# A two-block network on one core: the feed-forward norm's factor applied behind the second projection, rotary on wide tiles, no splits on GpSimd, a later merge, and the modulation rows spread differently

## The chip, the core and the metric

The kernel is one program on one core of one Trainium2 chip. The metric is the device time of one execution in microseconds (us), lower is better. The reported time is the median of the runs shown. One execution was also taken by the profiler; its own time and its span (first to last instruction) stand beside the median in the table below.

## What is computed

All tensors are float32, the sequence has 256 tokens and the width is 1024. Two networks follow each other.

```
# first block, twice (i = 0, 1)
z = rmsnorm(h, norm1[i]) @ w_in[i]                     # 1024 x 2560
q, k = partial rotary of the first 16 of 64 dims of each of 12 heads
h += concat(pool_mixer(u), dilated_attention(q, k, v)) @ w_out[i]
h += square(relu(rmsnorm(h, norm2[i]) @ w_up[i])) @ w_down[i]      # 1024 -> 4096 -> 1024
h += sigmoid(rmsnorm(h, norm3[i]) @ w_gate[i]) * (p[i] @ w_ple[i])
x = rmsnorm(h, final_norm)
# second block
mod   = silu(c)     @ w_mod + b_mod      # six parts of 1024: shifts, scales, gates
mod_c = silu(c_ctx) @ w_mod + b_mod      # only its parts 0 and 1 are used
h, hc = modulated norms of x (latent) and ctx (context), each @ w_in
context: gated delta rule in chunks of 64, both directions -> states
latent:  the same from these states -> o
merged = gate0 * (norm(o)*silu(z)) @ w_dn_out + gate1 * short_conv @ w_sc_out + gate2 * fourier @ w_fn_out
x += g1 * merged @ w_o
x += g2 * swiglu(modulated norm of x)
out = rmsnorm(x, final)
```

Since relu(r*y)^2 = r^2 * relu(y)^2 for r > 0, a norm's factor r of a token may be applied before the square, or as r^2 = 1/(mean square + eps) to the token's column of the second projection's result.

## The kernel before

**Products.** Float32 accuracy comes from splits: a matrix is cut into a high part in fp32r and the rest (`wh`, `wl` for weights, `xh`, `xl` for activations), and a product is three matmuls (`mm3`: high-high, high-rest, rest-high). A weight unit is 128 x 1024 (512 KB). `weights` (L250) loads it on SyncE's queue into `wst` (3 buffers), makes `wh` on ScalarE (L262) and `wl` on VectorE (L263), each as two halves of 512 columns. While `self.onpool` is above zero `wl` is made on GpSimd instead; the mixer sets it to `np2` = 3, so the first three weights of the mixer, six halves, go there. One unit feeds 24 matmuls of 256 columns.

**Order.** The program is written in one order, and the tile framework's list scheduler builds each engine's instruction stream from it: the traced order is the priority, an instruction that the scheduler's own model finds ready may be put ahead of earlier ones, and a tile needs a free buffer. Each engine then runs its stream strictly in order. `issue_after` puts an edge from an instruction to those traced in its block. A second stream is woven into the first by hand: `beside(gen, rate)` registers a generator, and each `tick` (one for each weight unit in `cols_into`, L664 and L672, and in a few other places) adds `rate` to a credit and takes one step of the generator for each whole credit. `drain` takes all that is left at once.

**Stages.** For i = 0, 1: attention (`proj`, `rotate`, `scores`, `softmax`, `av`, `pool`; no ticks), `ple`, the output projection `row_tiles`, `residual` (L699), `ffn(i)` (L706) and `gate(i)`. Then the mixer: value, query and key inputs of context and latent, `branches`, `dn_output`, the output products; then `swiglu` and `finish`.

**Feed-forward.** `ffn` splits h times its gain (`norm_split`, L297 and L298) without the norm's factor, so the first product can start at once. Meanwhile the factor's row is made in steps: the sum of squares (`sumsq`, ScalarE and VectorE), after the first unit the column sums on TensorE and a reciprocal root of ten small VectorE instructions (L345 to L361), after the third unit a transpose to a row `nrow`. From then on each pair of units f = 0..15 goes through `square`: relu and factor in one VectorE instruction for each half (L716), two squares on ScalarE (L719, L720), the rest on VectorE (L721). The second projection `down` runs one pair behind. At the end `residual` adds the four accumulators (256 columns x 2) to h in five VectorE instructions (L704), and `gate` begins with its own `norm_split` of h.

**Modulation.** `modulation` loads one 512 KB tile of `w_mod` (L878, pool `mp`, two buffers) and forms its row sums with one VectorE instruction of 1024 columns for each vector (L882): two vectors for parts 0 and 1, one for parts 2 to 5; eight tiles and nine steps for a part. Parts (1, 0, 2) are registered beside the first feed-forward at rate 0.85; parts (3, 4, 5) beside the latent's key and value inputs in the mixer at rate 0.8, and what is left there is woven with the recurrence. Its instructions carry an edge behind the last `shifted` one traced before, if there is one.

**Context and recurrence.** `context` runs beside the second feed-forward at rate 1.2, `recurrence` beside the branches at rate 0.8. In both, `dn_base` inverts 16 x 16 blocks on GpSimd, with trips through DRAM before and after (`there`, `back`, `xc`), then yields `self.trip` = 10 times, and `dn_merge` takes the result up (L1317, `Tm` and `U`).

Of the kernel before, what the change touches and what calls it, by code (L numbers as in the profile page):

```python
# [9 lines left out]
F32 = mybir.dt.float32  # L10
F32R = mybir.dt.float32r
I32 = mybir.dt.int32
AF = mybir.ActivationFunctionType
# [3 lines left out]
P = 128  # L17
# [177 lines left out]
def run(g):  # L195
    for _ in g:
        pass
# [33 lines left out]
class Net:  # L231
# [218 lines left out]
    def rotary(self):  # L450
# [28 lines left out]
        nc.scalar.activation(self.cos, t, AF.Sin)  # L479

# [29 lines left out]
    def rotate(self, z):  # L510
        nc = self.nc
        zz = z.rearrange("p t (h d) -> p t h d", d=HD)
        x1, x2 = zz[:, :, :, 0:8], zz[:, :, :, 8:16]
        co = self.cos[:, :, None, :].to_broadcast([P, 2, 8, 8])
        si = self.sin[:, :, None, :].to_broadcast([P, 2, 8, 8])
        w = [self.b1.tile([P, 2, 8, 8], F32, name=f"rot{j}", bufs=1) for j in range(4)]
        for o, x, c in zip(w, (x1, x2, x2, x1), (co, si, co, si)):
            for t in range(2):
                nc.vector.tensor_mul(o[:, t], x[:, t], c[:, t])
        for t in range(2):  # L520
            nc.vector.tensor_sub(x1[:, t], w[0][:, t], w[1][:, t])
            nc.vector.tensor_add(x2[:, t], w[2][:, t], w[3][:, t])
# [176 lines left out]
    def residual(self, acc):  # L699
        h = self.h  # L700
        for j in range(4):
            for n in ((0, 1), (1, 2)) if j == 3 else ((0, 2),):
                js = slice(2 * j + n[0], 2 * j + n[1])
                self.nc.vector.tensor_add(h[:, js], h[:, js], acc[j][:, n[0]:n[1]])  # L704

    def ffn(self, i):  # L706
        nc = self.nc
# [4 lines left out]

        def square(bv):
            t = self.sm.tile([P, 2, T], F32, name="fft", tag="w2k", bufs=self.nw2k)
            for n in range(2):
                nc.vector.scalar_tensor_tensor(t[:, n], bv[:, n], 0.0, r[0], op0=OP.max, op1=OP.mult)  # L716
            ah = self.sm.tile([P, 2, T], F32R, name="ah", tag="w2k", bufs=self.nw2k)
            al = self.sm.tile([P, 2, T], F32R, name="al", tag="w2k", bufs=self.nw2k)
            nc.scalar.activation(ah, t, AF.Square)  # L719
# [3 lines left out]

        r = []
        steps = self.row_steps_sb(self.h, r)
        next(steps)
        wait = []
        for f in range(16):
            bv = self.bank2()
            if f == 0 and self.ko & 4:  # L730
                self.cols_into(bv, [self.a["w_up"][i, n] for n in range(2)], x, True)
            for n in range(2):
                if f or not self.ko & 4:
                    self.cols_into(bv[:, n:n + 1], [self.a["w_up"][i, 2 * f + n]], x)
                if f == self.at[0] and n == self.at[1]:
                    next(steps)
                if f == self.at[2] and n == self.at[3]:
                    run(steps)
                    for b in wait:
                        square(b)  # L740
                    wait = None
            if wait is not None:
                wait.append(bv)
            else:
                square(bv)
                while len(pend) > 1:
                    down(False)
        self.residual(down(True))
# [57 lines left out]
    def layer(self, i):  # L806
# [38 lines left out]
        if i == 0:  # L845
            self.mod_setup()
            self.beside(self.modulation(*self.mod_parts[0]), 0.85)
# [72 lines left out]
    def context(self, d, e):  # L920
# [17 lines left out]
        yield from self.modulate(Halves(hc), self.gains[:, 1], self.mod[:, 0, 1], x)  # L938
# [836 lines left out]
    def run(self):  # L1775
# [5 lines left out]
        self.np1 = 3  # L1781
        self.np2 = 3
# [31 lines left out]
        self.trip = 10  # L1814
        self.mod_parts = (((1, 0, 2), (3,), (4, 5)), ((1, 0, 2), (), (3, 4, 5)), ((1, 0, 2, 3), (), (4, 5)), ((1, 0), (), (2, 3, 4, 5)))[1]
# [47 lines left out]
```

## Time and profile before

| | |
|---|---|
| median of 3 runs | 1226.24 us (1225.2 to 1228.88) |
| the profiled execution | 1224.34 us, span 1222.2 us |
| mean granted TensorE clock | 0.986 of full speed |
| TensorE busy, of the span | 1174.3 us, 96% |
| VectorE busy | 899.3 us, 74% |
| ScalarE busy | 635.6 us, 52% |
| GpSimd busy | 119.9 us, 10% |

How to read it: the busy time of an engine is the union of its instructions' intervals. A matmul's interval is longer than the distance to the next one, since they overlap, so a TensorE that is called busy can still run below its best rate; how many matmuls start in a stretch, and at which granted clock, says more.

### The profile page before, as it was taken

How to read it: one execution, taken by the hardware profiler on the slowest of the kernel's cores; microseconds unless marked ns; L12 is line 12 of the kernel's file. 1: busy time of each engine (PE TensorE's matmuls, PEld its weight loads, DVE VectorE, ACT ScalarE, POOL GpSimd, SP SyncE). 2: the span in 40 equal slices, each digit the busy share in tenths (PEclk: the TensorE clock that was granted, in tenths of full speed). 3: DMA queues.
4: the chain of work that ended last, by engine and by line, in shares of the span. 5: the costliest groups of instructions: out<-in, count | busy, mean ns of one | idle time of the engine just before them, and what ended most of it. 6: DMA issues, size and time to landing. Idle time of an engine off the chain costs nothing.

```text
span 1222.2 us, 24807 instructions
## 1 busy us (share of the span) xinstructions
PE 1174.3 (96%) x9882; PEld 1111.4 (91%) x9882; DVE 899.3 (74%) x1804; ACT 635.6 (52%) x1250; POOL 119.9 (10%) x207
## 2 busy tenths in 40 slices
PE   8999899999999989999999999997999999999997
PEld 6779899999977889999999979897989998999996
DVE  6998997556998488675657899897655768555555
ACT  5654645545755565644445555544333546544444
POOL 1000000000010000064000130275000000000000
PEclk9999999999999999999999989999999998999998
DMA  6767688555553645556444525677422452655552
GB/s 223 238 199 249 208 297 278 189 194 190 164 174 121 200 139 164 182 165 207 156 147 164 171 91 164 226 270 243 142 89 100 173 195 99 213 185 189 186 180 84
DMA packets 65779, 221.43 MB, mean 181 GB/s; under 512 B 10048, under 2 KB 11456, under 8 KB 65664
## 3 DMA queue, kind: packets, MB, share of 16 engines
q1 hardware_dynamic: 64800, 218.29, 53.4%
q0 software_dynamic: 864, 1.57, 0.6%
q8 instruction: 77, 1.26, 0.4%
q14 instruction: 38, 0.31, 0.1%
HBM read 218.00 MB, written 1.84 MB: 180 GB/s over the span
## 4 chain that ended last, share of the span: by engine, by line
PE 72%; DVE 13%; DMA 6%; POOL 4%; issue 3%; ACT 2%; SPq 0%; DVEq 0%; POOLq 0%; ACTq 0%
PE acc L274 38%; PE bank L274 33%; DVE wl L263 4%; DMA wmst<-w_mod 2%; DVE xl L298 1%; POOL bo L1288 1%; POOL bz L1289 1%; ACT wh L262 1%; DVE wmst L882 1%; PE bank L565 1%; DVE h L704 1%; DVE cy L1044 1%; DMA back<-bzt 1%; DVE qkT L533 1%; DMA pt<-pT 0%
## 5 line engine op out<-in xcount | busy, mean ns | idle before, releaser
L262 ACT ACTIVATE wh<-wst 128x512 fp32r<-128x512 f32 x708 | 411.9, 624 | 427.4 <-PE bank L274 157.3
L263 DVE TENSOR_TENSOR wl<-wst,wh 128x512 fp32r<-128x512 f32 x702 | 470.1, 703 | 208.5 <-ACT wh L262 208.0
L274 PE MATMUL bank<-xl,wh 128*128 128x256 f32 x992 | 280.5, 283 | 2.1 <-DVE xl L298 2.1
L274 PE MATMUL bank<-xh,wl 128*128 128x256 f32 x992 | 279.4, 282 | 2.9 <-DVE wl L263 2.9
L274 PE MATMUL bank<-xh,wh 128*128 128x256 f32 x992 | 281.3, 284 | 0.8 <-ACT wh L262 0.8
L274 PE MATMUL acc<-al,wh 128*128 128x256 f32 x688 | 191.6, 279 | 0.0
L274 PE MATMUL acc<-ah,wl 128*128 128x256 f32 x688 | 191.3, 279 | 0.0
L274 PE MATMUL acc<-ah,wh 128*128 128x256 f32 x688 | 191.2, 279 | 0.0
L274 PEld LDWEIGHTS bank<-xh,wl 128*128 128x128 f32 x992 | 187.0, 189 | 4.3 <-DVE wl L263 4.3
L274 PEld LDWEIGHTS bank<-xl,wh 128*128 128x128 f32 x992 | 187.0, 189 | 2.8 <-DVE xl L298 2.7
L274 PEld LDWEIGHTS bank<-xh,wh 128*128 128x128 f32 x992 | 187.1, 189 | 1.6 <-ACT wh L262 1.2
L274 PE MATMUL acc<-xh,wh 128*128 128x256 f32 x640 | 183.4, 287 | 2.2 <-ACT xh L911 2.2
L274 PE MATMUL acc<-xl,wh 128*128 128x256 f32 x640 | 182.0, 285 | 1.5 <-DVE xl L912 1.5
L274 PE MATMUL acc<-xh,wl 128*128 128x256 f32 x640 | 181.1, 284 | 0.5 <-DVE wl L263 0.4
L274 PEld LDWEIGHTS acc<-al,wh 128*128 128x128 f32 x688 | 129.0, 188 | 0.0
L274 PEld LDWEIGHTS acc<-ah,wl 128*128 128x128 f32 x688 | 128.9, 188 | 0.1
L274 PEld LDWEIGHTS acc<-ah,wh 128*128 128x128 f32 x688 | 128.9, 188 | 0.0
L274 PEld LDWEIGHTS acc<-xh,wh 128*128 128x128 f32 x640 | 121.6, 190 | 4.7 <-ACT xh L911 2.8
L274 PEld LDWEIGHTS acc<-xl,wh 128*128 128x128 f32 x640 | 121.5, 190 | 2.9 <-DVE xl L912 1.7
L274 PEld LDWEIGHTS acc<-xh,wl 128*128 128x128 f32 x640 | 121.9, 191 | 1.5 <-DVE wl L263 0.9
L274 PE MATMUL acc<-wl,xh 128*128 128x512 f32 x176 | 70.6, 401 | 2.5 <-DVE wl L263 2.4
L274 PE MATMUL acc<-wh,xh 128*128 128x512 f32 x176 | 70.8, 406 | 1.1 <-ACT wh L262 1.1
(365 smaller groups left out, 1564.8 us busy)
## 6 DMA issues: line engine op xcount, KB each, us to landing
wst<-w_up SPq DMA_DIRECT2D x64, 512.0 KB, 4.2
wst<-w_down SPq DMA_DIRECT2D x64, 512.0 KB, 4.2
wmst<-w_mod SPq DMA_DIRECT2D x48, 512.0 KB, 4.8
wst<-w_fin SPq DMA_DIRECT2D x44, 512.0 KB, 3.2
wst<-w_in SPq DMA_DIRECT2D x39, 512.0 KB, 3.6
wst<-w_mgate SPq DMA_DIRECT2D x24, 512.0 KB, 3.3
wst<-w_fout SPq DMA_DIRECT2D x22, 512.0 KB, 3.2
wst<-w_qkv SPq DMA_DIRECT2D x20, 512.0 KB, 3.4
```

What stands on the lines that cost most here:

```text
L262: nc.scalar.activation(wh[:, c:c + n], st[:, c:c + n], AF.Copy)
L263: i = (nc.gpsimd if self.onpool > 0 else nc.vector).tensor_tensor(wl[:, c:c + n], st[:, c:c + n], wh[:, c:c + n].bitcast(F32), op=OP.subtract)
L274: self.nc.tensor.matmul(out, lhsT, rhs, start=start, stop=stop, skip_group_check=skip)
L298: nc.vector.scalar_tensor_tensor(xl[:, k], src, gain, xh[:, k].bitcast(F32), op0=OP.mult, op1=OP.subtract)
L533: nc.vector.tensor_copy(qk[:, :, t * P:(t + 1) * P], bk.rearrange("p (c q) -> p c q", c=4))
L565: nc.tensor.transpose(bk[:, c * P:(c + 1) * P], s[:, g, c * P:(c + 1) * P], self.ident)
L704: self.nc.vector.tensor_add(h[:, js], h[:, js], acc[j][:, n[0]:n[1]])
L882: nc.vector.scalar_tensor_tensor(pr, st, 1.0, cv[v], op0=OP.mult, op1=OP.mult, accum_out=mod[:, part, v, k:k + 1])
L1044: nc.vector.scalar_tensor_tensor(y4[:, j], pad[:, j, :, tap:tap + CHUNK], w[:, j, tap:tap + 1], y4[:, j], op0=OP.mult, op1=OP.add)
L1288: pool.tensor_tensor(o, lt[:, c:, j:c].to_broadcast([P, n, c]), Z[:, j:c, 0:c].to_broadcast([P, n, c]), op=OP.mult)
L1289: pool.tensor_tensor(Z[:, c:, 0:c], Z[:, c:, 0:c], o, op=OP.subtract)
```

## The change

It does these things:

- `ffn` applies relu alone, on ScalarE, one instruction of 512 columns from PSUM; the squares and the rest are as before. The norm's steps start at f = 1 (sum of squares), 3 (mean square plus eps and its reciprocal) and 5 (transpose and copy to a row), and `residual` multiplies each accumulator by that row on VectorE before it adds.
- `rotary` builds two wide tables of 16 x 2 x 8 with eight VectorE instructions; `rotate` becomes three instructions of 256 columns in place of twelve of 64.
- `np2` is 0: no `wl` on GpSimd. (`np1` is read nowhere.)
- Modulation parts (1, 0, 2, 3) beside the first feed-forward at rate 0.55, parts (4, 5) behind the context, none in the mixer.
- `context` takes its sum of squares in its first step and then waits four steps before the rest of its norm.
- `trip` is 13.

```
--- before.py
+++ after.py
@@ -477,6 +477,13 @@
         nc.vector.scalar_tensor_tensor(t, r, -1.0, r, op0=OP.mult, op1=OP.max)
         nc.vector.tensor_scalar(t, t, -1.0, math.pi / 2, op0=OP.mult, op1=OP.add)
         nc.scalar.activation(self.cos, t, AF.Sin)
+        full = [self.b1.tile([P, 16, 2, 8], F32, name=n, bufs=1) for n in ("fcos", "fsin")]
+        for i in range(2):
+            for x in range(2):
+                for o, src, f in zip(full, (self.cos, self.sin), (1.0, 2.0 * x - 1.0)):
+                    nc.vector.tensor_scalar(o[:, 8 * i:8 * i + 8, x], src[:, i][:, None, :].to_broadcast([P, 8, 8]), f, None,
+                                            op0=OP.mult)
+        self.cos, self.sin = full
 
     def tokens_into(self, pt, x, q, w):
 
@@ -508,18 +515,13 @@
         return (z, r) if first else z
 
     def rotate(self, z):
-        nc = self.nc
-        zz = z.rearrange("p t (h d) -> p t h d", d=HD)
-        x1, x2 = zz[:, :, :, 0:8], zz[:, :, :, 8:16]
-        co = self.cos[:, :, None, :].to_broadcast([P, 2, 8, 8])
-        si = self.sin[:, :, None, :].to_broadcast([P, 2, 8, 8])
-        w = [self.b1.tile([P, 2, 8, 8], F32, name=f"rot{j}", bufs=1) for j in range(4)]
-        for o, x, c in zip(w, (x1, x2, x2, x1), (co, si, co, si)):
-            for t in range(2):
-                nc.vector.tensor_mul(o[:, t], x[:, t], c[:, t])
-        for t in range(2):
-            nc.vector.tensor_sub(x1[:, t], w[0][:, t], w[1][:, t])
-            nc.vector.tensor_add(x2[:, t], w[2][:, t], w[3][:, t])
+
+        nc = self.nc
+        zz = z.rearrange("p t (h d) -> p (t h) d", d=HD)[:, :, 0:16].rearrange("p n (x j) -> p n x j", x=2)
+        co, si = (self.b1.tile([P, 16, 2, 8], F32, name=f"rot{j}", bufs=1) for j in range(2))
+        nc.vector.tensor_mul(co, zz, self.cos)
+        nc.vector.tensor_mul(si, zz[:, :, ::-1], self.sin)
+        nc.vector.tensor_add(zz, co, si)
 
     def scores(self, i, b, z, S):
 
@@ -696,56 +698,61 @@
 
         return down
 
-    def residual(self, acc):
+    def residual(self, acc, row=None):
+
         h = self.h
         for j in range(4):
             for n in ((0, 1), (1, 2)) if j == 3 else ((0, 2),):
                 js = slice(2 * j + n[0], 2 * j + n[1])
-                self.nc.vector.tensor_add(h[:, js], h[:, js], acc[j][:, n[0]:n[1]])
+                a = acc[j][:, n[0]:n[1]]
+                if row is not None:
+                    t = self.t2k("fft")[:, n[0]:n[1]]
+                    self.nc.vector.tensor_mul(t, a, row[:, None, :].to_broadcast([P, n[1] - n[0], T]))
+                    a = t
+                self.nc.vector.tensor_add(h[:, js], h[:, js], a)
+
+    def mean_square_steps(self, h, res):
+
+        nc = self.nc
+        ss = self.sumsq(h)
+        yield
+        v = self.sm.tile([P, 2], F32, name="rsv2")
+        nc.vector.tensor_scalar(v, self.col_sums((ss,)), 1.0 / D, EPS, op0=OP.mult, op1=OP.add)
+        nc.vector.reciprocal(v, v)
+        yield
+        r = self.sm.tile([P, T], F32, name="nrow")
+        nc.scalar.activation(r, self.across(v)[:, 0:T], AF.Copy)
+        res.append(r)
 
     def ffn(self, i):
+
         nc = self.nc
         x = self.norm_split(self.h, lambda k: self.g2[:, i, k:k + 1])
         pend = []
 
         down = self.downward(self.a["w_down"][i], 32, pend)
-
-        def square(bv):
+        r = []
+        steps = self.mean_square_steps(self.h, r)
+        for f in range(16):
+            bv = self.bank2()
+            if f == 0 and self.ko & 4:
+                self.cols_into(bv, [self.a["w_up"][i, n] for n in range(2)], x, True)
+            else:
+                for n in range(2):
+                    self.cols_into(bv[:, n:n + 1], [self.a["w_up"][i, 2 * f + n]], x)
+            if f in (1, 3, 5):
+                next(steps, None)
             t = self.sm.tile([P, 2, T], F32, name="fft", tag="w2k", bufs=self.nw2k)
-            for n in range(2):
-                nc.vector.scalar_tensor_tensor(t[:, n], bv[:, n], 0.0, r[0], op0=OP.max, op1=OP.mult)
             ah = self.sm.tile([P, 2, T], F32R, name="ah", tag="w2k", bufs=self.nw2k)
             al = self.sm.tile([P, 2, T], F32R, name="al", tag="w2k", bufs=self.nw2k)
+            nc.scalar.activation(t, bv, AF.Relu)
             nc.scalar.activation(ah, t, AF.Square)
             nc.scalar.activation(t, t, AF.Square)
             nc.vector.tensor_sub(al, t, ah.bitcast(F32))
             pend.append((ah, al))
-
-        r = []
-        steps = self.row_steps_sb(self.h, r)
-        next(steps)
-        wait = []
-        for f in range(16):
-            bv = self.bank2()
-            if f == 0 and self.ko & 4:
-                self.cols_into(bv, [self.a["w_up"][i, n] for n in range(2)], x, True)
-            for n in range(2):
-                if f or not self.ko & 4:
-                    self.cols_into(bv[:, n:n + 1], [self.a["w_up"][i, 2 * f + n]], x)
-                if f == self.at[0] and n == self.at[1]:
-                    next(steps)
-                if f == self.at[2] and n == self.at[3]:
-                    run(steps)
-                    for b in wait:
-                        square(b)
-                    wait = None
-            if wait is not None:
-                wait.append(bv)
-            else:
-                square(bv)
-                while len(pend) > 1:
-                    down(False)
-        self.residual(down(True))
+            if f:
+                down(False)
+        self.residual(down(True), r[0])
 
     def ple(self, i):
         nc = self.nc
@@ -844,7 +851,7 @@
             return
         if i == 0:
             self.mod_setup()
-            self.beside(self.modulation(*self.mod_parts[0]), 0.85)
+            self.beside(self.modulation(*self.mod_parts[0]), 0.55)
         self.ffn(i)
         if self.stop == ("ffn", i):
             return
@@ -935,7 +942,11 @@
         nc.vector.tensor_scalar(self.k["dn_conv"], self.k["dn_conv"], 0.5, None, op0=OP.mult)
         yield
         x = self.xc = []
-        yield from self.modulate(Halves(hc), self.gains[:, 1], self.mod[:, 0, 1], x)
+        norm = self.modulate(Halves(hc), self.gains[:, 1], self.mod[:, 0, 1], x)
+        next(norm)
+        for _ in range(4):
+            yield
+        yield from norm
         yield
         yield from self.dn_inputs(x, True, d, e, ("k",), self.bank2)
         while d["late"]:
@@ -1778,8 +1789,8 @@
         self.side, self.rate, self.credit, self.busy = None, 0.0, 0.0, False
         self.dn_rate = 0.8
         self.hp = 0
-        self.np1 = 3
-        self.np2 = 3
+        self.np1 = 0
+        self.np2 = 0
         self.gadd = 0
         self.onpool = 0
         self.sy = 0
@@ -1811,8 +1822,8 @@
         self.ctx_rate = 1.2
         self.scan_rate = 1.8
         self.mod_rate = 0.8
-        self.trip = 10
-        self.mod_parts = (((1, 0, 2), (3,), (4, 5)), ((1, 0, 2), (), (3, 4, 5)), ((1, 0, 2, 3), (), (4, 5)), ((1, 0), (), (2, 3, 4, 5)))[1]
+        self.trip = 13
+        self.mod_parts = ((1, 0, 2, 3), (4, 5), ())
         with ExitStack() as ctx:
             self.ctx = ctx
             self.mp = ctx.enter_context(tc.tile_pool(name="mp", bufs=2, side="left"))
```

## Rows read from the trace of the kernel before

**Rows 1.** The page, part 1: busy time, share of the span, instructions.

```profile
PE 1174.3 (96%) x9882; PEld 1111.4 (91%) x9882; DVE 899.3 (74%) x1804; ACT 635.6 (52%) x1250; POOL 119.9 (10%) x207
```

**Rows 2.** Busy time by stretch: us, each engine (instructions), TensorE clock, DMA share, GB/s.

```profile
118.00:146.00 28.00, 23.62 (x185) 22.20 (x185) 26.95 (x60) 17.31 (x33) 0.00 (x0) 1.00 0.61 217
150.00:300.00 150.00, 149.57 (x1283) 149.36 (x1283) 103.66 (x183) 78.41 (x136) 0.00 (x0) 1.00 0.69 230
303.00:313.00 10.00, 9.54 (x81) 9.31 (x80) 9.72 (x21) 8.54 (x18) 0.00 (x0) 1.00 0.20 71
438.00:456.00 18.00, 13.98 (x100) 13.04 (x100) 17.04 (x50) 12.17 (x26) 0.00 (x0) 0.91 0.35 119
...
689.00:720.00 31.00, 25.91 (x190) 22.88 (x190) 26.94 (x63) 16.27 (x39) 16.81 (x30) 0.89 0.29 93
760.00:780.00 20.00, 17.09 (x121) 15.74 (x120) 17.38 (x43) 12.83 (x39) 1.37 (x4) 0.91 0.67 216
...
842.00:858.00 16.00, 10.26 (x118) 9.73 (x117) 9.21 (x21) 5.25 (x10) 3.28 (x4) 0.79 0.53 165
```

**Rows 3.** Waits of TensorE's matmuls: who for whom, us, times, longest.

```profile
PE bank L274 <- DVE U L1317: 5.4, 1, 5.4
...
PE bank L274 <- DVE rsy L358: 3.4, 1, 3.4
PE bank L370 <- DVE rsy L361: 3.1, 2, 1.9
PE bank L1143 <- DVE tokk L1134: 2.8, 1, 2.8
```

**Rows 4.** Timeline of VectorE at the first feed-forward's end: start, us, instruction.

```profile
307.33 0.74 DVE L704 TENSOR_TENSOR h<-h,acc 128x256 f32<-128x256 f32 x2
307.99 1.72 DVE L298 SCALAR_TENSOR_TENSOR xl<-h,k_norm,xh 128x256 fp32r<-128x256 f32 x4
309.62 0.69 DVE L317 TENSOR_TENSOR ssp<-sq 128x512 f32<-128x512 f32 x1
310.23 0.69 DVE L263 TENSOR_TENSOR wl<-wst,wh 128x512 fp32r<-128x512 f32 x1
```

**Rows 5.** Groups of instructions by line: count, busy us, mean ns, idle before.

```profile
L716 DVE SCALAR_TENSOR_TENSOR fft<-bank,nrow 128x256 f32<-128x256 f32 x64 | 24.4, 419 | 21.7 <-PE bank L274 21.4 <-ACT nrow L404 0.2
...
L519 DVE TENSOR_TENSOR rot<-zqk,rcos 128x64 f32<-128x64 f32 x24 | 5.3, 221 | 0.9 <-ACT zqk L507 0.8
...
L766 ACT ACTIVATE ple<-bank 128x512 f32<-128x512 f32 x8 | 4.8, 595 | 7.2 <-PE bank L274 7.2
```

**Rows 6.** Timeline of VectorE at the mixer's start.

```profile
694.56 0.16 DVE L359 SCALAR_TENSOR_TENSOR rst<-rsy 128x4 f32<-128x4 f32 x1
694.76 1.23 DVE L360 TENSOR_TENSOR rst<-rst,lv 128x4 f32<-128x4 f32 x1
...
714.17 2.88 DVE L1084 SCALAR_TENSOR_TENSOR vj<-cth,cy 128x256 f32<-128x256 f32 x2
```

**Rows 7.** Timeline of GpSimd at the mixer's start.

```profile
711.65 5.12 POOL L263 TENSOR_TENSOR wl<-wst,wh 128x512 fp32r<-128x512 f32 x2 [3.34 <-ACT wh L262]
```

**Rows 8.** Modulation tiles alone, by stretch: VectorE, ScalarE, clock, DMA share, GB/s.

```profile
60.00:118.00 58.00, 22.98 (x37) 0.00 (x0) 1.00 0.65 216
...
700.00:860.00 160.00, 30.51 (x48) 0.00 (x0) 0.95 0.59 197
```

**Rows 9.** The chain that ended last, around 759 us: start, us, what.

```profile
759.36 6.04 DMA wst<-w_z
```

**Rows 10.** The same chain between 838 and 858 us.

```profile
839.13 6.61 DMA back<-bzt
...
852.86 3.68 PE bank L274 x64
```

**Rows 11.** Timeline of ScalarE when the latent's recurrence has ended.

```profile
942.60 0.28 ACT L1123 ACTIVATE hsq<-acc 128x128 f32<-128x128 f32 x1 [2.99 <-PE acc L274]
```

**Rows 12.** Timeline of VectorE where that result is next multiplied.

```profile
973.44 1.41 DVE L1541 SCALAR_TENSOR_TENSOR do<-bank,k_onorm,zs 128x512 f32<-128x512 f32 x2 [1.46 <-PE bank L1539]
```

## The prediction, made before the change was built

> **What bounds the kernel now.** I read the page's busy times first: TensorE is busy 1174 of 1222.2 us, VectorE 74%, ScalarE 52% [rows 1]. So a VectorE instruction that goes is worth nothing in itself; only the places where TensorE stands still, or runs at a lower granted clock, can give time back. Next I read busy time by stretch to find these places [rows 2]. The reader should take one pitch from the steady feed-forward: 1283 matmuls start in 150 us, one each 0.117 us, so a weight unit of 24 takes 2.8 us. Held against that, 118 to 146 us has 185 matmuls, worth 21.6 us, in 28: 6.4 us lost. By the same sum 438 to 456 loses 6.3, 689 to 720 loses 8.8, and 760 to 780 loses 5.9. From 842 to 858 many matmuls are smaller, so there I read the idle time (16 − 10.26 = 5.7 us) and the clock, 0.79. All five stretches are touched by the change; in 150 to 300, where TensorE is busy 149.57 of 150 us, nothing is to be had. Third, TensorE's waits say what came last in these gaps: the merge's `U` 5.4 us, the column sums behind `rsy` at L358 3.4, the square root's end at L361 3.1 in two waits, and the token copy at L1134 2.8 [rows 3].
>
> **The change part by part.** The sum is made on the profiled execution's own 1224.34 us (span 1222.2 and 2.1 around it); the median of the runs is 1.9 above it, which is added at the end.
>
> 1. *Start of the second feed-forward.* The norm's ten small VectorE steps and the context's own wait behind each other in VectorE's queue (17.04 busy of 18 us), and TensorE waits 3.4 us there for `rsy` [rows 2, 3]. The change makes the row from two VectorE instructions, nothing in the first product needs it, and the context takes its norm four steps later. The wait can go, and with it the clock's loss, (1 − 0.91) × 18 = 1.6. Bounds −5.6 and −3.4 (the wait alone, without the 0.6 of idle time that is left and the clock); I take −5.
>
> 2. *Start of the first feed-forward.* TensorE idles 4.4 of 28 us at full clock [rows 2]. Of it the shorter of the L361 waits, 3.1 − 1.9 = 1.2 [rows 3], goes for certain; the rest stands behind VectorE (26.95 of 28 busy) and may go with eight instructions fewer. I take −2.5, between −1.2 and −4.4.
>
> 3. *End of each feed-forward.* `residual` gains a multiplication for each of its five adds. None like it is in the trace; the nearest rows are 0.37 for 128x256 (0.74 for two) and 0.69 for 128x512 [rows 4]. Both halves of the last accumulator give 0.74, all five 3 × 0.69 + 0.74 = 2.8. They stand ahead of the gate's split on a VectorE that is 9.72 of 10 us busy [rows 2]. What is late next is `xl` of the gate, then its first matmuls. I take +2.3 at each end, +4.6 together; at best the first four run while TensorE is at the last accumulator (0, since the adds are there now too), at worst 2.8 at each end, with a clock loss as in term 1: 2 × (2.8 + 1.6) = +8.8.
>
> 4. *Relu on ScalarE.* The 64 VectorE instructions of 0.419 us go; 32 on ScalarE come, which I price by the other ScalarE eviction of 128x512 from PSUM, 0.595 [rows 5]. ScalarE is busy 78 of 150 us [rows 2]; 32 × 0.595 = 19 us over two feed-forwards of some 165 us take it from 52% to 58%. TensorE covers it: 0. The Trainium skill has a rule against this edit: ScalarE: Activation LUTs, Rules for kernel authors, says to put relu on VectorE and not on ScalarE, since VectorE is up to about three times faster in bf16. No row here is in bf16; in float32 from PSUM the rows show 0.595 against 2 × 0.419 = 0.84, in ScalarE's favour. By the rows this term is 0; by the rule it would cost time, and that is a rival below.
>
> 5. *Rotary.* Twelve instructions of 128x64 at 0.22 become three of 128x256; 0.43 is the row for that width with two inputs [rows 4, 5]: 2.65 − 1.29 = 1.4 less at each of six calls. TensorE hardly waits there: −0.5, between 0 and −2. The setup gains eight instructions of 128x64, 8 × 0.22 = 1.8, at the start, where VectorE feeds the first products: +1, between 0 and +1.8.
>
> 6. *Mixer start, no splits on GpSimd.* Six halves of `wl` come to VectorE, 6 × 0.69 = 4.1, while it is 26.94 of 31 us busy [rows 2, 4]. What goes: a 128x4 instruction that takes 1.23 where its neighbour takes 0.16, and a pair of 128x256 that takes 2.88 where the same shape elsewhere takes 0.86 [rows 4, 6], so 1.1 + 2.0 = 3.1 of VectorE; and a `wl` half that takes GpSimd 2.56 comes in 0.69 [rows 4, 7]. VectorE's balance is +1, while the latency of six halves falls. I take −1.5, between −4 (half of the 8.8 lost) and +3 (4.1 less the 1.1 that surely goes).
>
> 7. *No modulation in the mixer.* Parts 3, 4, 5 took VectorE 30.5 us for 24 tiles between 700 and 860, with 12.6 MB of loads [rows 8]. From 760 to 780 TensorE idles 2.9 us and loses 1.8 by the clock [rows 2]; the token copy that it waits for 2.8 us [rows 3] stands behind a modulation instruction, and the chain runs through a `w_z` load of 6.04 us [rows 9]. I take −4, between 0 (the waits pass to other work) and −5.6 (2.8 + 2.8, wait and slow load both gone, about the 5.9 lost).
>
> 8. *Modulation beside the feed-forwards.* The 24 tiles must now fit earlier: 22 steps are taken in the first feed-forward (40 ticks × 0.55) of 36, the rest is drained behind it, and most of parts 4 and 5 are drained before the mixer, because the context's longer waits use up nearly all 40 ticks. The scheduler may float these tiles into any room: 9 of the present ones ran between 60 and 118 us, beside attention [rows 8], ahead of their tick. Steady VectorE is 69% busy and DMA 0.69 [rows 2], less 24.4 us of L716 [rows 5], which is most of the 30.5 that comes. I take +1.5, between 0 and +4 (three tiles of 1.27 that meet an edge between stages).
>
> 9. *Later merge.* Three more yields at rate 0.8 are 3.75 units, 10.5 us. `U` waits 5.4 us now [rows 3], behind a DRAM trip of 6.61 [rows 10], and the stretch loses (1 − 0.79) × 16 = 3.4 by the clock, seen in a block of 64 matmuls of 3.68 us [rows 2, 10]. Bounds −8.8 and 0 (the wait moves with the merge). At the other end the recurrence is later by 10.5 us; it ends at 942.6 [rows 11], and its result is next used at 973.4 [rows 12], 30.8 us of cover. Were it gone, all 10.5 would be paid. I take −6.5: the wait and a third of the clock.
>
> Sum: −5 − 2.5 + 4.6 + 0 − 0.5 + 1 − 1.5 − 4 + 1.5 − 6.5 = −12.9, so 1211.4 for a profiled run, and 1213 against the median.
>
> **The rivals.** *A, the mixer's waits only move:* TensorE at 840 us has then no other ready work, terms 6, 7 and 9 give 0 instead of −12. For it: the mixer's input has VectorE 87% busy even without `w_mod`. Against: the named releasers all go away. 1213 + 12 = 1225.
>
> *B, slower:* the modulation that is drained in the second layer doesn't float but runs where it is written. Some 13 tiles of 0.52 MB then stand on SyncE's queue ahead of the next stage's weights; at the 216 GB/s of the stretch where such tiles run now [rows 8] that is 6.8 MB in 31.5 us with TensorE starved, 1244. It decides where the drained tiles lie in a block with no weight loads between them. Against it: present tiles have run well ahead of their place [rows 8].
>
> *C, ScalarE becomes the bound in the feed-forward:* each relu then stands in TensorE's way, 32 × 0.595 = 19 us [rows 5], 1232. Against: 58% busy. The rule named in term 4 would speak for it.
>
> *D, the costs come out at their upper ends:* terms 3, 6 and 8 at +8.8, +3 and +4 add 11.2 to the sum, with the rest as forecast: 1224, no gain that can be seen.
>
> **How the numbers follow.** A measurement of this kernel can tell about 0.3%, 3.7 us, from no change: faster means below 1222.5, slower above 1230. Forecast 0.74; A 0.11; D 0.04; B 0.06; C 0.05. The forecast's own range: term 9 and term 7 at their ends give 1213 − 2.3 − 1.6 − 2.5 (term 6), some 1206, and together with terms 1 and 2 at their best 1203; upwards one of terms 7 or 9 at 0 gives 1217 to 1220. The range of 8 in 10 reaches to A, 1225, and leaves B, C and a small part below 1203. Faster takes the forecast, 0.74; A and D are the same, 0.15; B and C slower, 0.11.
>
> **What would show it.** Right: no wait for `rsy` at either feed-forward's start and the clock near 1.00 at 438 to 456; no wait over 1 us for `U`; 760 to 780 full; GpSimd without `wl`; ScalarE near 58% in the steady part with TensorE still at 149.5 of 150; up to 3 us of new idle time ahead of each gate. Wrong: a block of `wmst` loads without `wst` loads behind the second attention or before the mixer (B); TensorE's waits for `ah` (C); the mixer's five stretches with as many lost us, behind other releasers (A); or idle time where no modulation ran before, such as in attention.

## The result and the profile after

The changed kernel takes 1215.62 us (median, 1210.88 to 1217.01) against 1226.22 for the kernel before in the same sessions: a ratio of 0.9908, 95% interval 0.9885 to 0.9931. The forecast was 1213, range 1203 to 1225, faster at 0.74. Medians and ratios in this document leave out one slow execution, of the run e_norow (2282.70 us).

Page part 1 of the changed kernel:

```profile
PE 1171.1 (96%) x9882; PEld 1108.4 (91%) x9882; DVE 876.2 (72%) x1696; ACT 650.9 (54%) x1282; POOL 103.6 (9%) x201
```

Against [rows 1], VectorE lost 23 us and ScalarE won 15. Its busy time by stretch, in the stretches of [rows 2] and two more:

```profile
118.00:146.00 28.00, 26.76 (x224) 26.33 (x223) 26.33 (x49) 18.05 (x36) 0.00 (x0) 1.00 0.68 230
150.00:300.00 150.00, 146.63 (x1247) 145.60 (x1246) 100.11 (x168) 81.50 (x146) 0.00 (x0) 1.00 0.74 252
303.00:313.00 10.00, 7.80 (x62) 7.19 (x61) 9.96 (x22) 7.49 (x16) 0.00 (x0) 1.00 0.20 69
438.00:456.00 18.00, 18.00 (x154) 18.00 (x153) 15.44 (x29) 14.78 (x30) 0.00 (x0) 1.00 0.43 147
456.00:600.00 144.00, 139.79 (x1179) 137.40 (x1178) 110.38 (x219) 80.57 (x164) 42.79 (x80) 0.99 0.67 224
689.00:720.00 31.00, 27.41 (x219) 24.34 (x218) 25.43 (x73) 18.40 (x43) 7.15 (x24) 0.94 0.22 69
760.00:780.00 20.00, 18.99 (x169) 17.34 (x168) 15.96 (x47) 13.74 (x30) 1.78 (x4) 1.00 0.44 144
842.00:858.00 16.00, 16.00 (x186) 15.67 (x186) 11.20 (x23) 7.82 (x17) 0.00 (x0) 1.00 0.53 180
858.00:1010.00 152.00, 145.57 (x1452) 135.34 (x1448) 94.03 (x184) 66.44 (x146) 0.00 (x0) 1.00 0.36 120
```

The two new stretches in the kernel before:

```profile
456.00:600.00 144.00, 143.34 (x1227) 141.59 (x1226) 100.05 (x203) 78.61 (x157) 38.73 (x80) 1.00 0.55 174
858.00:1010.00 152.00, 152.00 (x1515) 142.46 (x1514) 97.06 (x185) 64.56 (x138) 0.00 (x0) 1.00 0.42 142
```

Count the matmuls that start. Won: 39 at the first feed-forward's start, 54 at the second's, 29, 48 and 68 in the mixer. Lost: 36 inside the first feed-forward, 19 at its end, 48 in the second beside the context, 63 from 858 to 1010. The balance is +72, at 0.117 us each 8.4 us; the spans differ by 8.5, and the stretches that aren't listed come to about +1 up to 1040 us. So some 28 us were won and 19 given back: the net says little of the parts.

The later stretches hold partly other work in the two kernels, so a single count there is rough. A second way doesn't depend on the edges: take all starts of matmuls in order of time and compare when the n-th starts in each profile. The 6600th starts 5.3 us earlier than in the kernel before, the 8400th 8.4 us. So the stretch from 842 to 1010 wins about 3 us, and not the 0.6 us of 68 less 63.

The changed kernel's waits of TensorE, and its waits for modulation tiles on VectorE and on ScalarE:

```profile
PE bank L274 <- DVE dr L1386: 4.5, 2, 2.3
...
PE bank L1124 <- DVE kT L1095: 3.4, 1, 3.4
...
PE bank L274 <- DVE xl L298: 1.9, 2, 1.7
DVE wmst L889 <- DMA wmst<-w_mod: 20.5, 15, 3.1
ACT wh L262 <- DVE wmst L889: 14.0, 6, 4.5
```

`U` and `rsy` at L358, the two longest of [rows 3], are gone. `dr` of the scan has grown from 0.4 to 4.5 us, and `kT` of the context is new. VectorE's 20.5 us were 5.4 before, ScalarE's 14.0 were 6.2. One such place, with SyncE's queue (the wait of its weight load stands in the second line), ScalarE, the chain of work, VectorE and TensorE:

```profile
162.61 0.33 SPq L256 DMA_DIRECT2D wst<-w_down  x1
SPq L256 <- DVE wl L263: 0.2, 1, 0.2
162.75 1.16 ACT L262 ACTIVATE wh<-wst 128x512 fp32r<-128x512 f32 x2 [1.86 <-DMA wst<-w_down]
168.40 1.87 ACT L262 ACTIVATE wh<-wst 128x512 fp32r<-128x512 f32 x3 [4.49 <-DVE wmst L889]
162.00 5.04 DMA wmst<-w_mod
167.13 1.23 DVE L889 SCALAR_TENSOR_TENSOR wmst<-wmst,cv 128x1024 f32<-128x1024 f32 x1 [1.61 <-DMA wmst<-w_mod]
168.29 2.50 DVE L263 TENSOR_TENSOR wl<-wst,wh 128x512 fp32r<-128x512 f32 x4
169.03 0.39 PE L274 MATMUL acc<-ah,wl 128*128 128x256 f32 x1 [1.00 <-DVE wl L263]
```

With two buffers, the load of the next `w_mod` tile is issued at 162.00, when VectorE has finished with an older tile, and it takes 5.04 us. The instruction on that tile stands in VectorE's order ahead of the next `wl` and waits 1.61 us for it. The `wh` halves of that `wl` begin at 162.75, but `wl` begins only at 168.29, and TensorE waits 1.00 us for it. The late `wl` also frees the weights' buffers late: the weight load at 162.61 waits for its own buffer, after the `w_mod` issue ahead of it is done, and lands at 168.3 (so ScalarE's 4.49 us end with this load as well as with `wmst`). SyncE's queue isn't what holds the weights: of 29 weight loads issued right behind a `w_mod` load from 146 to 300 and from 456 to 600 us, 28 waited for their own buffer after it.

From 456 to 600 us, 3.4 of the 4.2 us that TensorE idles are the wait for `kT`, which the context makes on VectorE. It is 0.3 us in e_mod and n1 below, where no modulation runs there.

### The profile page after: what moved, and what is told of

Same layout as the page of the kernel before. It is cut to its first block, busy times and chain, and to the rows that moved or that the text cites. A ratio compares the mean times of both kernels' runs of the same rounds, so it can differ in the third digit from the quotient of the medians.

```text
span 1213.7 us, 24726 instructions
## 1 busy us (share of the span) xinstructions
PE 1171.1 (96%) x9882; PEld 1108.4 (91%) x9882; DVE 876.2 (72%) x1696; ACT 650.9 (54%) x1282; POOL 103.6 (9%) x201
## 4 chain that ended last, share of the span: by engine, by line
PE 62%; DVE 13%; issue 12%; DMA 7%; POOL 4%; ACT 2%; SPq 0%; DVEq 0%; POOLq 0%; ACTq 0%
PE acc L274 37%; PE bank L274 23%; DMA wmst<-w_mod 5%; DVE wl L263 4%; DVE wmst L889 1%; ACT wh L262 1%; DVE cy L1055 1%; DMA wst<-w_in 1%; PE bank L567 1%; POOL bo L1299 1%; DVE xl L298 1%; POOL bz L1300 1%; DVE S L546 0%; DVE qkT L535 0%; DMA there<-ac 0%
## 5 line engine op out<-in xcount | busy, mean ns | idle before, releaser
L263 DVE TENSOR_TENSOR wl<-wst,wh 128x512 fp32r<-128x512 f32 x708 | 475.2, 702 | 217.5 <-ACT wh L262 212.9
L889 DVE SCALAR_TENSOR_TENSOR wmst<-wmst,cv 128x1024 f32<-128x1024 f32 x48 | 58.4, 1224 | 20.7 <-DMA wmst<-w_mod 20.5
```

The costliest lines, as they stand in the source:

```text
L263: i = (nc.gpsimd if self.onpool > 0 else nc.vector).tensor_tensor(wl[:, c:c + n], st[:, c:c + n], wh[:, c:c + n].bitcast(F32), op=OP.subtract)
L889: nc.vector.scalar_tensor_tensor(pr, st, 1.0, cv[v], op0=OP.mult, op1=OP.mult, accum_out=mod[:, part, v, k:k + 1])
```

## The experiments

Unless said otherwise, each is the changed kernel with one edit. Ratios are to the kernel before, with 95% intervals; "costs" compares medians with 1215.62. The runs were taken in several sessions, in which the kernel before had medians from 1226.07 to 1228.68, so differences of 2 us between medians of two sessions stand for little.

**e_ffn: the old feed-forward.** `ffn` as before, `residual` without the row.

> The changed kernel with the old feed-forward: the factor's row ahead of the squares, relu and factor in one VectorE instruction of each half, no multiplication in the residual. Theory: the starts of the two feed-forwards lose again what they won (4.8 and up to 6.4 us, the second part only if the context's later norm isn't enough by itself), the first end wins 2.3 us: 5 to 9 us slower, 1220 to 1225. Rival: the context's later norm alone removed the second start's wait, and only the first start is lost: 4.8 - 2.3 = 2.5 us slower, 1218.

1219.6 us, 0.9943 (0.9922 to 0.9964): the new feed-forward is worth some 4 us, though the intervals touch. The two starts:

```profile
118.00:146.00 28.00, 24.04 (x185) 23.36 (x185) 26.60 (x58) 14.78 (x29) 0.00 (x0) 0.94 0.61 205
...
438.00:456.00 18.00, 15.85 (x120) 15.14 (x120) 17.09 (x45) 12.66 (x25) 0.00 (x0) 0.94 0.43 145
```

The first start falls back to 185, all 39 matmuls. The second keeps 20 of its 54 and loses 34, which are the feed-forward's. The 20 come from other parts of the change, by their place from the context's later norm, which wasn't tried alone. Even with the old feed-forward the wait of 3.4 us for `rsy` at L358 doesn't come back; TensorE's longest wait there is 1.7 us, for a `wh`.

**e_norow: no multiplication in the residual.** `self.residual(down(True))`.

> The changed kernel without the multiplication by the norm's row in the residual: the factor is left out of the second projection's result (its row is still made). Theory: the five multiplications cost 2.3 us at the first feed-forward's end (1.9 of them TensorE's wait for xl of the gate) and about nothing at the second: 1213, with 15 more matmuls started by 316 us. Rival: they cost 2.3 at both ends: 1211. Other rival: they lie under the last accumulator's products, and the later start of the gate has another cause: 1215.

```profile
303.00:313.00 10.00, 9.54 (x81) 9.31 (x80) 9.24 (x19) 8.56 (x19) 0.00 (x0) 1.00 0.32 105
```

81 matmuls again, as in [rows 2], against 62: the multiplications do cost 19 × 0.117 = 2.2 us at the first end. At the second, the changed kernel loses nothing: its one long wait for `xl` (1.7 us) is at the first. The time, 1215.65 and 0.992 (0.9892 to 0.9948), doesn't resolve 2 us.

**e_relu: relu on VectorE.** `nc.vector.tensor_scalar(t, bv, 0.0, None, op0=OP.max)`.

> The changed kernel with relu as one VectorE instruction of 512 columns in place of one on ScalarE. Theory: ScalarE at 55% in the steady feed-forward has room and VectorE with the modulation beside it has less, so relu on VectorE makes wl later still: 146 to 300 us starts under 1282 matmuls, 1 to 4 us slower, 1217 to 1220. The rule that relu belongs on VectorE would make it faster by up to 32 x 0.6 = 19 us if ScalarE set the pace. Rival: neither engine sets the pace, 1215 to 1216.

1216.81 us, 0.9919 (0.9891 to 0.9946): the rival, no difference that can be seen. One relu of 128x512 takes 583 ns on ScalarE (first line, the changed kernel) and 689 ns on VectorE:

```profile
L748 ACT ACTIVATE fft<-bank 128x512 f32<-128x512 f32 x32 | 18.7, 583 | 1.7 <-PE bank L274 1.7
...
L748 DVE TENSOR_SCALAR fft<-bank 128x512 f32<-128x512 f32 x32 | 22.0, 689 | 16.6 <-PE bank L274 16.5
```

Neither engine sets the pace. The Trainium skill (ScalarE: Activation LUTs, Rules for kernel authors) puts relu on VectorE, which it calls up to about 3 times faster in bf16. No run here is in bf16; for this shape in float32 from PSUM the measured order is the other way, 689 against 583 ns.

**e_mod: the modulation's old places.**

```
-        self.beside(self.modulation(*self.mod_parts[0]), 0.55)
-        self.mod_parts = ((1, 0, 2, 3), (4, 5), ())
+        self.beside(self.modulation(*self.mod_parts[0]), 0.85)
+        self.mod_parts = ((1, 0, 2), (), (3, 4, 5))
```

> The changed kernel with only the modulation put back: parts 1, 0, 2 beside the first feed-forward at rate 0.85, parts 3, 4, 5 in the mixer. Theory: the 24 tiles cost the feed-forwards more than the 1.5 us forecast; from 146 to 300 us the changed kernel starts 35 matmuls fewer (1282 against 1317, 4.1 us at 0.117 each) and from 456 to 600 48 fewer (5.6 us). Put back, both losses go (over 1305 matmuls in 146 to 300), and the mixer loses its 3 to 4 us at 760 to 780 again: 4 to 7 us faster than the changed kernel, some 1209 to 1212. Rival: the losses come from the new feed-forward's own order and the context's later norm, and stay, while the mixer loses 4 us or more: 1219 or above.

1218.64 us, 0.9941 (0.9922 to 0.9961): a cost of 3, though the intervals touch, so neither theory's time. Its place-by-place part was right:

```profile
150.00:300.00 150.00, 149.45 (x1281) 149.19 (x1280) 92.86 (x153) 82.52 (x148) 0.00 (x0) 1.00 0.66 228
...
456.00:600.00 144.00, 143.00 (x1220) 140.83 (x1220) 93.51 (x184) 82.14 (x167) 39.32 (x80) 1.00 0.54 178
...
842.00:858.00 16.00, 16.00 (x195) 15.64 (x196) 12.73 (x27) 8.80 (x19) 0.00 (x0) 1.00 0.65 210
```

The stretches start 1281 and 1220 matmuls again, 75 more in all or 8.8 us, and yet the time isn't better: the mixer loses about as much. In this profile the 5000th matmul starts 8.4 us earlier than in the changed kernel, and the 7000th only 0.4 us earlier. The last row shows that with 13 yields the gap at 842 stays closed even with modulation in the mixer.

**e_trip10: the merge back at 10 yields.** `self.trip = 10`.

> The changed kernel with the merge back at 10 yields. Theory: the later merge took the wait of 842 to 858 away, but gave most of it back at 890 to 912, where TensorE now waits twice for the scan (2.3 and 2.2 us for dr): by matmul counts 842 to 858 won 68 matmuls and 858 to 1010 lost 63, so the net worth of the merge is about nothing to 4 us: 1215 to 1220. Rival: the merge is worth its forecast 6.5 us or more, since without it the U wait of 5 us comes back and the recurrence still runs late: 1222 or above. Other rival: without modulation in the mixer the DRAM trip is over by the tenth yield, no U wait comes back, and trip 10 is faster than trip 13 by the 4.5 us of dr waits: 1211.

1214.65 us, 0.9914 (0.9886 to 0.9941): no difference.

```profile
842.00:858.00 16.00, 16.00 (x228) 15.60 (x227) 11.17 (x24) 7.49 (x15) 0.00 (x0) 1.00 0.48 166
858.00:1010.00 152.00, 150.96 (x1454) 141.33 (x1453) 95.94 (x184) 68.66 (x151) 0.00 (x0) 1.00 0.38 129
```

No gap at 842, and idle time from 858 to 1010 falls from 6.4 to 1.0 us: the second rival's mechanism. Its gain is not in the time. `trip` also moves the context's merge, and in this profile 456 to 600 us starts 1165 matmuls, 14 fewer, at a clock of 0.98, and 600 to 689 us 959 in place of 977. Held against the changed kernel, the 3500th matmul is 1.0 us late, the 6000th 5.6 and the 8500th 1.1: 4.6 us are lost around the context's merge and 4.5 won back around the latent's. That the loss comes from the context's merge was not tried apart, but n5 below keeps the context at 13.

**e_pool: the splits back on GpSimd.** `self.np2 = 3`.

> The changed kernel with the first three weights of the mixer split on GpSimd again (six halves). Theory: contention of VectorE with GpSimd made a 128x4 instruction take 1.23 us and a 128x256 pair 2.88; these come back, and 689 to 720 starts some 20 to 29 matmuls fewer than 219: 2 to 4 us slower, 1218 to 1220. Rival: VectorE, with no modulation beside it, has room, and the mixer's start is set by the chain of the norm: within 1 us of 1215.6, with a long VectorE instruction again but no later matmuls.

1228.38 us, 1.001 (0.9989 to 1.0031): a cost of 12.8 us, far above either theory.

```profile
689.00:720.00 31.00, 27.22 (x179) 26.00 (x178) 21.90 (x56) 16.99 (x39) 12.45 (x27) 0.78 0.30 99
...
858.00:1010.00 152.00, 147.56 (x1471) 136.37 (x1471) 91.31 (x173) 61.42 (x131) 0.00 (x0) 0.96 0.36 123
```

The held-up instructions are there, as the first four `mt` show in the kernel before, the changed kernel and e_pool:

```profile
700.55 2.76 DVE L996 SCALAR_TENSOR_TENSOR mt<-h,lgg,lrows 128x128 f32<-128x128 f32 x4
...
703.24 1.95 DVE L1007 SCALAR_TENSOR_TENSOR mt<-h,lgg,lrows 128x128 f32<-128x128 f32 x4
...
708.05 2.74 DVE L1007 SCALAR_TENSOR_TENSOR mt<-h,lgg,lrows 128x128 f32<-128x128 f32 x4
```

TensorE waits 2.0 and 1.5 us for `xh` and `xl` of the modulated input. But the larger part goes with the clock: as an estimate, a mean of 0.978 over 1229.5 us against 0.989 over 1213.7 makes 27.05 − 13.35 = 13.7 of the 15.8 us between the spans. This profile is the slowest of ten runs; over all runs the mean clocks are 0.981 and 0.989, and the fastest of the ten, 1221.55 us, is still slower than every run of the changed kernel. By the n-th matmul, 2.0 of the 15.8 us are lost ahead of the mixer, where this edit changes nothing, some 7 up to 870 us, and 5.6 at the two `dr` waits (0.83 from 900 to 920 us), which can cost clock without the splits too (n3 below). So the splits' own share of the 13.7 us isn't known.

**b_pool: the kernel before, with only `np2 = 0`.**

> The kernel before with one part of the change alone: no weight splits on GpSimd at the mixer's start. Putting them back into the changed kernel cost some 12 us, with the granted clock at 0.78 in 689 to 720 us. Theory: these splits alone hold up VectorE's short instructions and the late wl halves at the mixer's start, so that TensorE rests and its clock falls; done alone the part gives most of it: 1216 to 1220. Rival: in the kernel before the mixer is bound by the modulation on VectorE, which has to take the six halves too, so the part alone gives under 4 us: 1222 to 1226, and it is worth 12 us only after the modulation has left.

1222.19 us, 0.9962 (0.994 to 0.9984): some 4.8 us, between the savings of the two theories (its time is at the edge of the rival's range). In its profile 689 to 720 us stays at a clock of 0.89, with 203 matmuls in place of 190, and 760 to 780 us goes from 121 to 143.

**e_poolmod: both of e_mod's lines and `np2 = 3`.**

> The changed kernel with two parts put back together: the six weight splits on GpSimd and the modulation's old places. Alone the first cost 12.8 us and the second 3; in the kernel before, taking the splits off GpSimd gave 4.8. Theory: what the splits cost depends on what else stands in the mixer; with the modulation there the cost is the 4.8 of the kernel before, and the two together make 1215.6 + 3 + 4.8 = 1223. Rival: the splits cost 12.8 beside the new feed-forward or the later merge, whatever the modulation does: 1231.

1220.68 us, 0.9962 (0.9934 to 0.9991), only 2 above e_mod. The rival falls: by the medians the splits cost 12.8 where the modulation has left the mixer, and 2 to 5 where it hasn't.

```profile
689.00:720.00 31.00, 25.10 (x197) 21.40 (x197) 26.57 (x57) 19.73 (x46) 16.91 (x32) 0.96 0.26 83
```

TensorE is idle longer here than in e_pool (5.9 against 3.8 us), yet at 0.96 and not 0.78. Why the same splits bring the clock down in one order and not in the other isn't settled by these runs.

**e_mp3r: three buffers for `w_mod`.** The pool `mp` gets `bufs=3` on the other side of the memory.

> The changed kernel with three buffers for the w_mod tiles in place of two (the pool moved to the other side of the memory, where it is given up before the mixer). Theory: beside the feed-forward a w_mod instruction stands in VectorE's queue until its load lands, since with two buffers the load is issued only behind the instruction two before; VectorE waits 20.5 us in all for these loads and the weights' wl behind it are late. With a third buffer the wait for w_mod falls to some 5 us or less, 146 to 300 us starts 1300 matmuls or more in place of 1282, and the time falls by 2 to 5 us: 1211 to 1213. Rival: the loads are limited by the transfers (0.74 of the DMA's time in that stretch), so the third buffer only takes the weights' share, ScalarE waits for weights more, and nothing is won: 1214 to 1217.

```profile
150.00:300.00 150.00, 149.99 (x1281) 149.48 (x1280) 102.61 (x171) 81.81 (x147) 0.00 (x0) 1.00 0.74 257
```

and its wait of VectorE for the tiles:

```profile
DVE wmst L889 <- DMA wmst<-w_mod: 12.0, 10, 2.1
```

The stretch is full again with the same DMA share, which speaks for the number of buffers as its limit and against the transfers (e_relu, with two buffers and another order on VectorE, came near it with 1277). The wait of 12.0 us is still above the 5 expected, and the wait for `kT` beside the context stays at 3.1 us. The time, 1215.63 and 0.9905 (0.9867 to 0.9943), is the same: the 4 us are lost again later, with 0.83 clock at 303 to 313 and 0.98 from 858 on.

**n1 and n3: the modulation where there is room.** Both chain the late parts behind the recurrence in place of weaving them with it, and take part 5 in `swiglu`. The expectation of n3 speaks of two buffers for `w_mod`, but its kernel has the pools of n1: three buffers until the mixer, two new ones from there. The main lines, others left out (`...`):

```
+        self.beside(chain(recurrence(), self.modulation(*self.mod_parts[2])), self.dn_rate)
...
+            if f == 1:
+                self.beside(self.modulation(*self.mod_parts[3]), 0.5)
...
+            self.mp = b1p.enter_context(tc.tile_pool(name="mp", bufs=3, side="right"))
...
+            self.mp = ctx.enter_context(tc.tile_pool(name="mp2", bufs=2, side="right"))
# n1, rate 0.55 as in the changed kernel:
+        self.mod_parts = ((1, 0, 2, 3), (), (4,), (5,))
# n3, rate 0.85:
+        self.mod_parts = ((1, 0, 2), (), (3, 4), (5,))
```

> A new version: the changed kernel with three buffers for w_mod until the mixer; parts 1, 0, 2, 3 beside the first feed-forward as in it, nothing behind the context, part 4 behind the recurrence (beside the branches' end, two buffers of its own), part 5 beside the last block's feed-forward. Theory: the modulation beside the context is what takes 48 matmuls from 456 to 600 us (5.6 us), and the recurrence's end and the last block have room (VectorE under 62% busy, DMA under 0.46): 4 to 7 us faster than the changed kernel, 1209 to 1212. Rival: the context's loss is its own (the wait for kT comes from the padding on GpSimd) and stays, and part 4's eight tiles stand ahead of the recurrence's output: 1214 to 1217.

> A second new version: the changed kernel with two buffers for w_mod; parts 1, 0, 2 beside the first feed-forward at the old rate 0.85, nothing behind the context, parts 3 and 4 behind the recurrence, part 5 beside the last block's feed-forward. Theory: both feed-forwards run as smoothly as before (1317 matmuls in 146 to 300 us, 1227 in 456 to 600), and sixteen tiles fit at the branches' end, where VectorE is 62% busy: 5 to 9 us faster than the changed kernel, 1207 to 1211. Rival: sixteen tiles are too many between the recurrence's end near 930 and the last block's start at 1005; they delay the output's VectorE work: 1215 to 1222.

n1 takes 1215.03, 0.9905 (0.988 to 0.9931), no gain, though its theory was right on the place: 456 to 600 us starts 1216 matmuls, and the wait for `kT` is 0.3 us. n3 takes 1211.32, 0.9874 (0.9846 to 0.9901), just above its theory; its interval touches that of the changed kernel. n3's stretches:

```profile
150.00:300.00 150.00, 150.00 (x1293) 150.00 (x1293) 94.90 (x156) 82.86 (x150) 0.00 (x0) 1.00 0.67 221
...
456.00:600.00 144.00, 143.00 (x1220) 140.82 (x1220) 92.94 (x179) 83.67 (x169) 39.15 (x80) 1.00 0.55 175
...
880.00:900.00 20.00, 17.85 (x156) 15.81 (x155) 7.77 (x13) 5.35 (x11) 0.00 (x0) 0.83 0.16 53
900.00:920.00 20.00, 17.71 (x170) 15.62 (x170) 12.01 (x21) 4.75 (x11) 0.00 (x0) 0.91 0.23 80
```

Both feed-forwards are smooth. In the first, e_mod has 1281 matmuls with two buffers, so most of the gain over 1247 comes with the old parts and rate; what the third buffer adds here isn't separated. The modulation written behind the recurrence doesn't run there: its tiles (8 in n1, 16 in n3) lie between 689 and 860 us. And the two `dr` waits now cost clock too.

**n5: n3 with 10 yields for the latent.** `self.trip = 10` at the mixer's start.

> The version n3 with the merge of the latent's recurrence back at 10 yields, the context's left at 13. Theory: with the modulation out of the mixer the DRAM trip is over by the tenth yield (the changed kernel with 10 yields throughout shows neither a wait for U nor the two dr waits, and runs 820 to 985 us without idle time at full clock); with 13 the scan meets the branches' end with too little beside it, waits 2.3 and 2.2 us for dr, and in n3 the clock falls to 0.83 and 0.91 there. So 858 to 1010 us wins 4.4 us of waits and up to 7 of clock: 1203 to 1208. Rival: the merge at 10 only moves the same wait, as in the changed kernel, where 10 and 13 yields gave the same time: 1210 to 1213.

1207.77 us, 0.9832 (0.981 to 0.9853), the best of all and inside its theory; its interval lies below that of the changed kernel, though it touches n3's. It has n3's buffers.

```profile
880.00:900.00 20.00, 20.00 (x184) 17.16 (x184) 11.21 (x23) 9.21 (x21) 0.00 (x0) 1.00 0.17 54
900.00:920.00 20.00, 20.00 (x214) 18.25 (x214) 12.78 (x22) 5.48 (x12) 0.00 (x0) 1.00 0.33 106
```

and among TensorE's waits:

```profile
PE bank L274 <- DVE U L1328: 2.9, 2, 2.7
```

The `dr` waits and their clock loss are gone. A `U` wait of 2.7 us has come back, so the rival was half right. With 16 tiles still between 689 and 860 us, ten yields seem slightly too few; that wasn't tried further.

## Why the prediction was right, by its own steps

The time came out within 2.6 us of the forecast. No modulation block was starved on the queue (B), and ScalarE, 54% busy from 150 to 300 us, wasn't the bound (C). Rival A, that the mixer's waits only move, came true for the merge alone: its wait passed from `U` to `dr`. One sign of being right failed: TensorE is busy 146.63 of 150 us in the steady part, not 149.5. The sum came out by errors that cancel, so that it lies this near is partly luck.

- Terms 1 and 2, the starts: forecast −5 and −2.5; by matmuls −6.3 and −4.6. Right in place, undersized; both pass their bounds, −5.6 and −4.4. Of term 1's 54 matmuls 34 are the feed-forward's (e_ffn). The wait for `rsy`, which term 1 priced, stays away in e_ffn too, so another part of the change is enough to remove it.
- Term 3, the residual: +2.3 at the first end, measured 2.2. No wait at the second, where +2.3 was forecast.
- Term 4, relu: 0, as e_relu bears out within its noise; the price was 0.595, measured 0.583. Term 5: the wide rotary instructions take 0.42 against the 0.43 taken, the setup 0.19 each; not tried by itself.
- Term 6, the splits, failed in size: −1.5, at most −4, was forecast from the busy time and the latency of six halves. Alone it gave 4.8; put back into the changed kernel it cost 12.8, with a mean clock of 0.981 against 0.989. The sum listed 3.1 us of held-up VectorE work and not the `mt` (2.76 against 1.95 us), and it priced no change of the clock.
- Terms 7 and 8, the modulation: −4 and +1.5 forecast, −2.5 together; e_mod gives −3, which its interval doesn't tell from 0. Right as a sum, and by luck, since both are mis-sized. Term 8: 84 matmuls, 9.8 us, are lost in 150 to 300 and 456 to 600, and e_mod gives 75 of them back. Term 7: the mixer takes 8.0 us more with the modulation in it (e_mod, from the 5000th to the 7000th matmul), past its bound of −5.6. Term 8 was worked out from busy shares (69% and 0.69), where the limit is VectorE's order: a `w_mod` tile that comes late, with two buffers, holds up `wl` in the first feed-forward, and the modulation delays `kT` in the second.
- Term 9, the merge, failed: −6.5 forecast, 0 measured (e_trip10). The wait for `U` did go, but without the modulation in the mixer it goes at ten yields too, and with 13 yields it goes with the modulation there (e_mod): one gain with two causes was booked in full on one. And the cover of 30.8 us was counted from the recurrence's end to the next use of its result; the later scan costs earlier, inside the recurrence, where TensorE waits 4.5 us for `dr` between 880 and 920 us.

The parts do not add: undone one at a time, feed-forward, modulation, splits and merge cost 4.0 + 3.0 + 12.8 − 1.0 = 18.8 us, and together 10.6. With the splits at their worth alone, 4.8, the sum is 10.8; each part is uncertain by some 3 us (half its interval), so the agreement may be chance.

## What to carry to other kernels

Filler work is not free where an engine has idle time: look at which instructions stand behind it in its engine's order, and at whether its own load has landed when its turn comes. If two edits remove the same wait, book it once, and follow a delayed chain to its last consumer and count what is left to run beside it. Idle time is not the whole price of a wait: in e_pool 3.8 us of it go with a clock of 0.78 over 31 us.

## What the runs showed of the hardware

The clock's price for a wait isn't fixed. Two `dr` waits, 4.5 us together, cost no clock in the changed kernel's profile:

```profile
880.00:900.00 20.00, 17.64 (x214) 15.91 (x213) 9.90 (x18) 5.97 (x13) 0.00 (x0) 1.00 0.20 68
900.00:920.00 20.00, 17.50 (x179) 15.76 (x178) 11.86 (x21) 5.94 (x11) 0.00 (x0) 1.00 0.23 80
```

With waits of 4.4 us the same two stretches show 0.83 and 0.91 in n3, 1.00 and 0.83 in e_relu, and 0.91 and 1.00 in e_mp3r. That, and the 1236 to 1259 matmuls that start from 150 to 300 us in four kernels with the same feed-forward there (e_trip10, e_norow, e_pool and the changed kernel), may be why single runs of one kernel lie up to 10 us apart (e_pool's from 1221.55 to 1231.24); that link wasn't tried. Effects of 3 us had to be read from their places, and not from times alone.
